# Input products that start before the normalisation, and PSUM banks in two sets of four

## The chip, the cores and the metric

One core of a Trainium2 chip runs the whole program in one launch. The metric is device time in microseconds (us), the median of several executions; lower is better.

## The reference, cut to what matters

Two stacked networks of two layers each work on 1024 tokens of 1024 channels, all in fp32. The change touches the first layer and, through the PSUM banks, every stage.

```
h    = x * rsqrt(mean(x*x, -1) + 1e-6) * norm_w        # RMS norm, per token
proj = h @ w_in                                        # q, k, v, z, q_h, f_h, i_h, g_h, gates
q, k = partial_rope(q), partial_rope(k)                # tables cos, sin from positions
a    = sliding_window_attention(q, k, v, sinks) * silu(z)
b    = hgrn2_recurrence(silu(q_h), f_h, i_h) -> norm -> * silu(g_h)
x    = x + (sigmoid(ga)*(a @ w_up_attn) + sigmoid(gh)*(b @ w_up_hgrn)) @ w_out
```

This layer runs twice. Then follow a gated MLP layer with a spatial mix in groups of 128 tokens, and a chunked attention layer in which each block of queries sees up to 640 keys with a relative bias. Since `norm_w` belongs to channels and the root to tokens, `h @ w` equals `((x * norm_w) @ w)` with each token's row multiplied by its own factor afterwards.

## The kernel before, in words

**Numbers.** A product of two fp32 tensors is made of three matmuls in the format fp32r: each operand is split into a high part (a cast) and a low part (operand minus high part), and high x high, high x low and low x high are accumulated in PSUM.

**Layout.** x and h lie channel-major: 8 tiles (index k) of 128 channels by tokens, in two halves of 512 tokens. A *unit* is one weight block with its products. `unit` (L252) and `unit_wide` (L279) work on 512 columns; `unit_tok` (L265) is token-major: h is the stationary operand, the output has 128 tokens by 256 columns, and one tile takes 24 matmuls (8 k times 3). `load_w` (L243) fetches a weight block by the SP queue into one of three `raw` buffers (`fetch_w`, L214), then `split_w` (L223) makes the parts `wh` and `wl`, of which there are 8 each.

**Order.** `run_units` (L297) writes the program unit by unit; the weights of a unit are requested two units ahead. Small work (rotary embedding, attention, recurrence, later norms) sits in *fibers*, Python generators. `tick` (L321) counts the matmuls that were written, and after each 24 of them `step` (L332) lets every fiber advance to its next `yield`. `finish` (L353) runs fibers to their end. The compiler then orders each engine's instructions by program order and readiness in its own model; TensorE's order stays nearly that of the program. `after` (L413) chains instructions behind given ones of the same engine. Copies and subtractions without a named engine go to the engine with the least booked load.

**PSUM.** Eight banks of 128 x 512 fp32 values. `mm` (L144) takes one for a unit's product, `aux` (L147) for everything else; both draw on one tag with eight buffers. `heap` (L135) gives one of 61 SBUF tiles of 128 x 512.

**The start.** `load_first` (L1139) works on the first half of the tokens in two quarters of 256, from `xq`, whose tiles hold two k each. SP fetches four x tiles, the first weight block (keys and values) in two transfers, then the second quarter's four x tiles. `squares(0)` (L1152) squares on ScalarE, adds on VectorE and sums over channels on TensorE by a matrix of ones (L1163); `rstd_of` (L386) makes the root on ScalarE and its reciprocal with one correction step on VectorE. Chained behind the root, the first weights are split on ScalarE and GpSimd; `scale(0)` (L1166) multiplies x by gain and factor and splits the result; `squares(1)` and its root follow.

**The first units.** In `layer_a` (L836) the first unit's `run` (L933) makes keys and values (`kvwork`) and the first query group (`qwork[0]`) for token tiles 0 and 1, then calls `second` (L1192), which normalises the second quarter and writes the rotary tables and constants, chained behind what ScalarE and VectorE have then, and goes on with token tiles 2 and 3. Then come the second query group (token-major), V of the recurrence (`wide_unit` with L289 to L291), and `head(0)`, whose products are L261 to L263. `swa_kv` (L545) copies keys and values out of PSUM; its fiber rotates the keys (`rope`, L529), splits them into `khl` and transposes them on TensorE (L573). The tables come from `rope_angles` (L421: a position transfer on ScalarE's queue, some forty small VectorE steps), `rope_tables` (L459) and `first_constants` (L481, three mask transfers on ScalarE's queue). `swa_q` (L593) scales queries by 1/8 as it copies them out.

**Chunked attention.** `attn2` (L1329) makes blocks of 128 queries for two heads: scores into two or four banks (L1424), VectorE's bias and maximum out of them, ScalarE's exponential, transposes (L1460), and the product with V (L1470) into one bank, which ScalarE copies out (L1476).

Of the kernel before, what the change touches and what calls it, by code (L numbers as in the profile page):

```python
# [96 lines left out]
class Net:  # L97
# [167 lines left out]
    def unit_tok(self, ps, lhs, w, t, n):  # L265
# [4 lines left out]
        for k in range(KD):  # L270
# [6 lines left out]
            nc.tensor.matmul(ps, ll[:, o : o + P], wh[:, c : c + n], start=False, stop=(k == KD - 1))  # L277

# [265 lines left out]

    def swa_kv(self, st, t, pskv):  # L545
# [6 lines left out]
        nc.scalar.copy(out=X, in_=pskv[:, 0:128])  # L552
        nc.scalar.copy(out=st["v"][:, o : o + P], in_=pskv[:, 128:256])
# [39 lines left out]
    def swa_q(self, st, l, kv, t, psq):  # L593
# [3 lines left out]
        self.nc.scalar.activation(out=X, in_=psq[:, 0:256], func=AF.Copy, scale=0.125)  # L597
# [238 lines left out]
    def layer_a(self, l, half, h, carry, merged, ready, early=None, first=None):  # L836
# [3 lines left out]
              "kvf": [], "wait": FWAIT if first else 0, "qf": [], "hf": []}  # L840
# [4 lines left out]
        def tok_unit(ap, work):  # L845
            def run(w):
                for t in range(4):
                    ps = self.mm()
                    self.unit_tok(ps[:, 0:256], h, w, 4 * half + t, 256)
                    work(4 * half + t, ps)  # L850
                    self.tick(12)
            self.units.append((lambda: self.load_w(ap, 2048), run))

        def wide_unit(ap, work):
            self.units.append((lambda: self.load_w(ap, 4096), lambda w: self.unit_wide(h, w, half, work)))

        def vwork(t, ps):
            st["V"][t] = self.heap()
            nc.scalar.copy(out=st["V"][t], in_=ps)
# [67 lines left out]
        else:  # L927

            def load():
                with self.after(first[1]):  # L930
                    return first[0], self.load_w(a["w_tok"][l, 1], 2048)

            def run(w):  # L933
                for q in range(2):
# [11 lines left out]
        wide_unit(a["w_wide"][l, 1], vwork)  # L946
        head(0)
# [191 lines left out]
    def load_first(self, res):  # L1139
# [3 lines left out]
        xs = [self.heaps(KD // 2) for _ in range(2)]  # L1143
        for k in range(KD // 2):
            nc.sync.dma_start(out=xs[0][k], in_=self.a["xq"][0, k])
        raws = self.fetch_w(self.a["w_tok"][0, 0], 2048)
# [568 lines left out]
```

## Time and profile before

| | |
|---|---|
| median of 3 runs | 3022.28 us (3022.23 to 3022.83) |
| the profiled execution | 3024.32 us |
| its span, first to last instruction | 3022.5 us |
| TensorE's mean granted clock | 0.990 of full speed |
| TensorE (PE) busy | 97% of the span |
| VectorE (DVE), ScalarE (ACT), GpSimd (POOL) busy | 56%, 48%, 36% |
| HBM read and written | 259.66 and 20.97 MB |

PE is TensorE's matmul, PEld its load of the stationary operand, SPq and ACTq a queue that issues transfers. All of the kernel's calls on VectorE, ScalarE and GpSimd go through one wrapper, so they stand under one line, L76, and are told apart by their tiles: `hp` a heap tile, `raw`, `wh`, `wl` weights, `mm` and `aux` PSUM banks. One fp32 matmul that isn't fp32r appears as two hardware matmuls, a transpose as one. A busy time that is longer than the distance to the next start means that the next instruction was already running into the pipeline: distances between starts give the pace.

### The profile page before, as it was taken

The numbers are of one execution on the slowest core, as the hardware profiler recorded it, in microseconds if no ns is written. First come the engines' busy times: TensorE is split into PE (matmuls) and PEld (weight loads), VectorE is DVE, ScalarE is ACT, GpSimd is POOL, SyncE is SP. The second block draws the span as 40 slices with busy tenths as digits, with TensorE's granted clock in tenths as the row PEclk, the third lists the DMA queues.
The fourth block names the chain that finished last, engine by engine and source line by source line (L and its number), as shares of the span: only waits on it lengthen the run. The fifth ranks groups of instructions, "written<-read, shape, count | busy, mean of one in ns | idle before, by whom it ended". The sixth has DMA issues, their size and how long they took to land.

```text
span 3022.5 us, 43638 instructions
## 1 busy us (share of the span) xinstructions
PE 2927.0 (97%) x16188; PEld 2432.3 (80%) x16188; DVE 1678.1 (56%) x3298; ACT 1449.5 (48%) x2927; POOL 1091.5 (36%) x1174
## 2 busy tenths in 40 slices
PE   6999999999999999999999999999999799999997
PEld 5887887888878888788888878888888688878777
DVE  6556745556556666665666533445344644454566
ACT  4665325642357434475334455334544545564552
POOL 4445333543435433444332233213332322232331
PEclk9999999999999999999999999999999899999999
DMA  3212242122522224212243222533234111111123
GB/s 113 84 63 93 89 147 82 66 70 91 182 70 71 73 84 151 99 70 70 74 151 132 101 92 97 166 103 129 95 116 159 56 38 60 38 59 44 64 98 112
DMA packets 101493, 283.47 MB, mean 94 GB/s; under 512 B 11288, under 2 KB 15512, under 8 KB 101280
## 3 DMA queue, kind: packets, MB, share of 16 engines
q1 hardware_dynamic: 100016, 279.51, 27.3%
q8 instruction: 128, 2.10, 0.3%
q10 hardware_dynamic: 1264, 1.17, 0.1%
q14 instruction: 85, 0.70, 0.1%
HBM read 259.66 MB, written 20.97 MB: 93 GB/s over the span
## 4 chain that ended last, share of the span: by engine, by line
PE 89%; DVE 4%; issue 2%; POOL 2%; DMA 1%; ACT 1%; SPq 0%; DVEq 0%; POOLq 0%; ACTq 0%
PE mm L261 20%; PE mm L262 20%; PE mm L263 20%; PE mm L289 3%; PE mm L290 3%; PE mm L291 3%; DVE hp L76 3%; PE aux L703 2%; PE aux L1470 2%; PE aux L1424 2%; PE mm L275 2%; PE aux L1460 2%; PE mm L276 1%; PE mm L277 1%; PE aux L634 1%
## 5 line engine op out<-in xcount | busy, mean ns | idle before, releaser
L261 PE MATMUL mm<-hp,wh 128*128 128x512 f32 (+1 forms) x2816 | 1118.8, 397 | 0.0
L262 PE MATMUL mm<-hp,wh 128*128 128x512 f32 (+1 forms) x2816 | 1093.2, 388 | 2.0 <-POOL hp L76 2.0
L263 PE MATMUL mm<-hp,wl 128*128 128x512 f32 (+1 forms) x2816 | 1093.7, 388 | 0.0
L76 POOL TENSOR_TENSOR wl<-raw,wh 128x512 fp32r<-128x512 f32 x369 | 491.3, 1334 | 800.7 <-ACT wh L76 690.7
L76 ACT CAST wh<-raw 128x512 fp32r<-128x512 f32 x584 | 360.4, 620 | 692.5 <-PE mm L262 467.1
L76 POOL TENSOR_TENSOR hp<-hp,hp 128x256 f32<-128x256 f32 (+3 forms) x347 | 380.5, 1102 | 680.1 <-DVE hp L76 240.3
L261 PEld LDWEIGHTS mm<-hp,wh 128*128 128x128 f32 x2816 | 530.7, 188 | 114.9 <-issue 11.2
L263 PEld LDWEIGHTS mm<-hp,wl 128*128 128x128 f32 x2816 | 530.0, 188 | 110.9 <-issue 0.2
L262 PEld LDWEIGHTS mm<-hp,wh 128*128 128x128 f32 x2816 | 531.1, 189 | 102.0 <-POOL hp L76 3.3
L76 DVE TENSOR_TENSOR wl<-raw,wh 128x512 fp32r<-128x512 f32 x447 | 358.8, 805 | 231.8 <-ACT wh L76 188.7
L76 DVE TENSOR_TENSOR hp<-hp,hp 128x512 f32<-128x512 f32 (+2 forms) x407 | 296.3, 737 | 154.9 <-ACT hp L76 109.3
L76 ACT ACT_TABLE_LOAD x244 | 313.1, 1283 | 22.9 <-PE mm L263 10.5
L76 DVE TENSOR_TENSOR hp<-mm,hp 128x512 f32<-128x512 f32 (+2 forms) x264 | 166.6, 637 | 161.1 <-ACT hp L76 79.3
L76 ACT ACTIVATE hp<-mm 128x512 f32<-128x512 f32 (+2 forms) x304 | 171.4, 574 | 170.0 <-PE mm L291 78.8
L76 DVE CAST wh<-raw 128x512 fp32r<-128x512 f32 x232 | 118.9, 513 | 186.9 <-PE mm L262 148.9
L76 ACT CAST hp<-hp 128x512 fp32r<-128x512 f32 (+1 forms) x206 | 116.0, 574 | 217.9 <-POOL hp L76 179.8
L76 POOL TENSOR_SCALAR sP<-sP,a2l 128x640 f32<-128x640 f32 (+4 forms) x128 | 89.0, 697 | 284.4 <-DVE a2l L76 176.7
L289 PE MATMUL mm<-wh,hp 128*128 128x512 f32 x480 | 188.1, 392 | 0.0
L290 PE MATMUL mm<-wl,hp 128*128 128x512 f32 x480 | 188.1, 392 | 0.0
L291 PE MATMUL mm<-wh,hp 128*128 128x512 f32 x480 | 187.8, 391 | 0.0
L76 ACT ACTIVATE sP<-sP,a2nm 128x640 f32<-128x640 f32 (+4 forms) x128 | 88.3, 691 | 101.1 <-DVE a2nm L76 101.0
L275 PE MATMUL mm<-wh,hp 128*128 128x256 f32 x448 | 133.7, 298 | 0.0
(186 smaller groups left out, 3406.0 us busy)
## 6 DMA issues: line engine op xcount, KB each, us to landing
raw<-in_w_ch_dram SPq DMA_DIRECT2D x128, 512.0 KB, 3.3
raw<-in_g_uz_dram SPq DMA_DIRECT2D x64, 512.0 KB, 3.3
hp<-xd SPq DMA_DIRECT2D x88, 256.0 KB, 4.2
raw<-in_w_up_dram SPq DMA_DIRECT2D x64, 256.0 KB, 2.7
raw<-in_w_o_dram SPq DMA_DIRECT2D x32, 512.0 KB, 3.3
raw<-in_g_v_dram SPq DMA_DIRECT2D x32, 512.0 KB, 4.0
raw<-in_g_o_dram SPq DMA_DIRECT2D x32, 512.0 KB, 3.8
raw<-in_w_wide_dram SPq DMA_DIRECT2D x28, 512.0 KB, 3.9
```

What stands on the lines that cost most here:

```text
L76: self.last = f(*args, **kw)
L261: nc.tensor.matmul(ps, wh[:, c : c + P], rh, start=(k == 0), stop=False)
L262: nc.tensor.matmul(ps, wh[:, c : c + P], rl, start=False, stop=False)
L263: nc.tensor.matmul(ps, wl[:, c : c + P], rh, start=False, stop=(k == nk - 1))
L275: nc.tensor.matmul(ps, lh[:, o : o + P], wh[:, c : c + n], start=(k == 0), stop=False)
L289: nc.tensor.matmul(ps, lh[:, s], wh, start=(k == 0), stop=False)
L290: nc.tensor.matmul(ps, lh[:, s], wl, start=False, stop=False)
L291: nc.tensor.matmul(ps, ll[:, s], wh, start=False, stop=(k == KD - 1))
L703: nc.tensor.matmul(ps[:, s], k[:, s], q[:, s], start=True, stop=True)
L1424: nc.tensor.matmul(ps[:, 0:w], lhs[r, o : o + P], rhs[r, k0 : k0 + w], start=(j == 0), stop=(j == 2))
L1460: nc.tensor.transpose(ps[:, j * P : (j + 1) * P], S[:, (i + j) * P : (i + j + 1) * P], self.ident)
L1470: nc.tensor.matmul(po[e * 64 : e * 64 + 64, 0:P], vv, pts[e][:, i * P : (i + 1) * P], start=(i == 0), stop=(i == nb - 1),)
```

## The change

All 8 banks were shared; now `mm` has four and `aux` has four. `load_first` no longer normalises. It makes `raw_h`, the split product of x and the gain, per quarter (`part`), interleaves the weight transfers with those of x, and returns closures. `columns(q)` puts the sum of squares per token into one PSUM column per token tile and makes the factor `rs`, and `rs8`, which is an eighth of it, with tokens on the partitions. `second` makes the second quarter's parts and squares, `constants` the rotary tables and constants. `normalise` is a fiber that makes the normalised `h` as before, for the units from `head(0)` on. The first unit works on pairs of token tiles (`pair_tok`). The first four groups of products (keys and values, both query groups, V) read `raw_h`, and `leave` multiplies by the token's factor as ScalarE copies out. A unit that finishes `normalise` stands ahead of `head(0)`.

```diff
     def mm(self):
-        return self.ps.tile([P, H], F32, tag="bank", bufs=8, name=self.name("mm"))
+        return self.ps.tile([P, H], F32, tag="mm", bufs=4, name=self.name("mm"))
     def aux(self):
-        return self.ps.tile([P, H], F32, tag="bank", bufs=8, name=self.name("aux"))
+        return self.ps.tile([P, H], F32, tag="aux", bufs=4, name=self.name("aux"))
...
+    def pair_tok(self, pss, lhs, w, ts, n):
...
+        for k in range(KD):
+            wh, wl = w[k // kg]
+            c = slice((k % kg) * n, (k % kg) * n + n)
+            for ps, t in zip(pss, ts):
+                s = slice((t % 4) * P, (t % 4) * P + P)
+                lh, ll = lhs[k][t // 4]
+                nc.tensor.matmul(ps, lh[:, s], wh[:, c], start=(k == 0), stop=False)
+                nc.tensor.matmul(ps, lh[:, s], wl[:, c], start=False, stop=False)
+                nc.tensor.matmul(ps, ll[:, s], wh[:, c], start=False, stop=(k == KD - 1))
...
+    def leave(self, st, t, out, ps):
+        if st["rs"] is None:
+            self.nc.scalar.copy(out=out, in_=ps)
+        else:
+            self.nc.scalar.activation(out=out, in_=ps, func=AF.Copy, scale=st["rs"][:, t % 4 : t % 4 + 1])
...
-        nc.scalar.copy(out=X, in_=pskv[:, 0:128])
-        nc.scalar.copy(out=st["v"][:, o : o + P], in_=pskv[:, 128:256])
+        self.leave(st, t, X, pskv[:, 0:128])
+        self.leave(st, t, st["v"][:, o : o + P], pskv[:, 128:256])
...
-        self.nc.scalar.activation(out=X, in_=psq[:, 0:256], func=AF.Copy, scale=0.125)
+        scale = 0.125 if st["rs"] is None else st["rs8"][:, t % 4 : t % 4 + 1]
+        self.nc.scalar.activation(out=X, in_=psq[:, 0:256], func=AF.Copy, scale=scale)
...
             def load():
-                with self.after(first[1]):
-                    return first[0], self.load_w(a["w_tok"][l, 1], 2048)
+                return first["w"], self.load_w(a["w_tok"][l, 1], 2048)
             def run(w):
                 for q in range(2):
-                    if q:
-                        first[2]()
-                    for wi, work in zip(w, (kvwork, qwork[0])):
-                        for t in (2 * q, 2 * q + 1):
-                            ps = self.mm()
-                            self.unit_tok(ps[:, 0:256], h, wi, t, 256)
+                    for i, (wi, work) in enumerate(zip(w, (kvwork, qwork[0]))):
+                        ts = (2 * q, 2 * q + 1)
+                        pss = [self.mm() for _ in ts]
+                        self.pair_tok([ps[:, 0:256] for ps in pss], ht, wi, ts, 256)
+                        if i == 0:
+                            first["columns"](q)
+                        for t, ps in zip(ts, pss):
                             work(t, ps)
                             if q:
                                 self.tick(12)
+                        if q == 0 and i == 0:
+                            first["second"]()
+                        if q == 0 and i == 1:
+                            first["constants"]()
+                norm = self.spawn(first["normalise"]())
+                st["norm"].append(norm)
...
         wide_unit(a["w_wide"][l, 1], vwork)
+        if first:
+            self.units.append((None, lambda w: self.finish(st["norm"])))
...
         for k in range(KD // 2):
             nc.sync.dma_start(out=xs[0][k], in_=self.a["xq"][0, k])
-        raws = self.fetch_w(self.a["w_tok"][0, 0], 2048)
+            if k % 2 == 0:
+                raws += self.fetch_w(ap[:, k * 512 : k * 512 + 1024], 1024)
...
+        def part(q, k):
+            gain = self.col("norm_w", k)
+            hi, lo = (t[:, q * Q : q * Q + Q] for t in raw_h[k][0])
+            nc.scalar.activation(out=hi, in_=view(q, k), func=AF.Copy, scale=gain)
+            nc.vector.scalar_tensor_tensor(
+                out=lo, in0=view(q, k), scalar=gain, in1=hi.bitcast(F32), op0=ALU.mult, op1=ALU.subtract
+            )
...
+        def columns(q):
+            ps = self.aux()
+            for t in range(2):
+                for i in range(2):
+                    s = i * Q + t * P
+                    nc.tensor.matmul(
+                        ps[:, t : t + 1], accs[q][:, s : s + P], self.ones_f[:, 0:1], start=(i == 0), stop=(i == 1)
+                    )
+            r = rs[:, 2 * q : 2 * q + 2]
...
+            nc.vector.tensor_scalar(out=v, in0=ps[:, 0:2], scalar1=EPS, scalar2=None, op0=ALU.add)
+            nc.scalar.activation(out=r, in_=v, func=AF.Sqrt)
+            nc.vector.reciprocal(r, r)
...
+            nc.vector.tensor_scalar(out=rs8[:, 2 * q : 2 * q + 2], in0=r, scalar1=0.125, scalar2=None, op0=ALU.mult)
+        w = []
+        for k in range(KD):
+            part(0, k)
+            if k % 4 == 0:
+                w += self.split_w(raws[k // 4], 0, None, False, ("scalar", "gpsimd"))
+        squares(0)
         def second():
-            scale(1, r)
+            for k in range(KD):
+                part(1, k)
+            squares(1)
+        def constants():
             with self.after((nc.scalar.last, nc.vector.last)):
                 self.rope_angles()
                 self.rope_tables()
                 self.first_constants()
-        return w, last, second
+        def normalise():
+            for q in range(2):
+                ps = self.aux()[:, :Q]
+                for i in range(2):
+                    nc.tensor.matmul(ps, self.ones_f, accs[q][:, i * Q : (i + 1) * Q], start=(i == 0), stop=(i == 1))
+                r = self.rstd_of(ps, Q)
+                yield
+                for k in range(KD):
+                    x = view(q, k)
+                    nc.vector.scalar_tensor_tensor(
+                        out=x, in0=x, scalar=self.col("norm_w", k), in1=r, op0=ALU.mult, op1=ALU.mult
+                    )
+                    if q == 0:
+                        res[k][0] = self.pair()
+                    hi, lo = (t[:, q * Q : q * Q + Q] for t in res[k][0])
+                    self.split(x, hi, lo)
+                    if k % 4 == 3:
+                        yield
```

In the middle of `columns`, where the diff is cut, five VectorE steps on 128 x 2 values make one correction step of the reciprocal root. `ht` is `raw_h` for the first half of the first layer and `h` everywhere else; the units of keys and values, of queries and of V read it.

## Rows read from the trace of the kernel before

**Rows 1.** The page: busy us (share of the span) and instructions of TensorE.

```profile
PE 2927.0 (97%) x16188; PEld 2432.3 (80%) x16188; DVE 1678.1 (56%) x3298; ACT 1449.5 (48%) x2927; POOL 1091.5 (36%) x1174
```

**Rows 2.** Windows: length, PE, PEld, DVE, ACT, POOL busy (count), PEclk, DMA share, GB/s.

```profile
0.00:28.60 28.60, 3.52 (x8) 2.35 (x9) 17.80 (x30) 13.90 (x27) 13.72 (x18) 1.00 0.51 177
28.60:59.50 30.90, 30.90 (x243) 30.81 (x241) 23.24 (x74) 13.51 (x36) 11.81 (x26) 1.00 0.29 93
59.50:68.00 8.50, 3.89 (x23) 2.91 (x22) 6.80 (x17) 4.29 (x23) 7.57 (x17) 0.74 0.21 76
```

**Rows 3.** Waits of TensorE over the span: us in total, times, longest us.

```profile
PE aux L1163 <- DVE hp L76: 25.1, 2, 17.4
...
PE aux L573 <- POOL khl L76: 7.6, 5, 3.0
```

**Rows 4.** Timeline to 33 us: start us, us, engine, line, operation, tiles, count.

```profile
6.27 0.63 ACT L76 ACTIVATE hp<-hp 128x512 f32<-128x512 f32 x1 [0.61 <-DMA hp<-in_xq_dram]
...
9.79 0.47 ACT L76 ACTIVATE hp<-aux,eps 128x256 f32<-128x256 f32 x1 [2.89 <-PE aux L1163]
10.16 2.16 ACT L76 CAST wh<-raw 128x512 fp32r<-128x512 f32 x4
...
10.86 5.29 POOL L76 TENSOR_TENSOR wl<-raw,wh 128x512 fp32r<-128x512 f32 x4 [9.54 <-ACT wh L76]
...
22.13 0.73 POOL L76 TENSOR_TENSOR hp<-hp,hp 128x256 fp32r<-128x256 f32 x1 [0.80 <-ACT hp L76]
...
27.15 2.08 PE L1163 MATMUL aux<-hp,ones_f 128*128 128x256 f32 x4 [17.40 <-DVE hp L76]
...
28.67 0.78 PE L275 MATMUL mm<-wh,hp 128*128 128x256 f32 x1
...
32.86 0.28 PE L275 MATMUL mm<-wh,hp 128*128 128x256 f32 x1
...
32.98 0.28 PE L276 MATMUL mm<-wl,hp 128*128 128x256 f32 x1
```

**Rows 5.** Windows of the first 10 us, columns as in rows 2.

```profile
0.00:5.00 5.00, 0.00 (x0) 0.00 (x0) 0.98 (x8) 2.74 (x4) 0.71 (x6) 1.00 0.65 216
5.00:10.00 5.00, 2.07 (x4) 1.17 (x4) 2.08 (x3) 1.47 (x4) 0.00 (x0) 1.00 0.98 320
```

**Rows 6.** Timeline from 39 to 68 us: positions, rotary tables, split keys, the next product.

```profile
39.17 0.35 ACTq L426 DMA_DIRECT2D pos<-in_pos_dram  x1
...
54.56 0.33 DVE L76 TENSOR_SCALAR cos<-angn 128x64 f32<-128x64 f32 x2
...
65.44 1.72 POOL L76 TENSOR_TENSOR khl<-hp,khl 128x128 fp32r<-128x128 f32 x4
...
67.75 0.54 PE L275 MATMUL mm<-wh,hp 128*128 128x256 f32 x1
```

**Rows 7.** Timelines from 86 to 103 us, engine by engine.

```profile
86.60 0.46 PE L614 MATMUL aux<-identr,hp 128*128 128x128 f32 x4
...
92.86 1.29 POOL L76 TENSOR_TENSOR wl<-raw,wh 128x512 fp32r<-128x512 f32 x1 [0.49 <-ACT wh L76]
...
93.10 1.33 DVE L76 CAST wh<-raw 128x512 fp32r<-128x512 f32 x1 [2.07 <-PE mm L291]
...
99.16 0.41 DVE L76 CAST wh<-raw 128x512 fp32r<-128x512 f32 x1
...
102.65 0.40 PE L261 MATMUL mm<-hp,wh 128*128 128x512 f32 x1
```

**Rows 8.** Timeline of one block of the chunked attention, from 2621 to 2625 us.

```profile
2621.49 1.09 PE L1470 MATMUL aux<-pT,hp 128*64 128x128 f32 x16
...
2622.52 1.15 PE L1424 MATMUL aux<-hp,hp 64*128 64x256 f32 x12
2622.63 0.27 ACT L76 COPY hp<-aux 128x128 f32<-128x128 f32 x1 [0.66 <-PE aux L1470]
...
2624.45 0.55 DVE L76 CUSTOM_DVE_ANT_0 sP<-aux,bias 128x384 f32<-128x384 f32 x1
```

More of the change, by code (lines that the diff above doesn't have):

```diff
@@ L839, in layer_a @@
               "b32": [None] * 4, "o": [None] * 4, "V": [None] * 4, "carry": carry,
-              "kvf": [], "wait": FWAIT if first else 0, "qf": [], "hf": []}
+              "kvf": [], "wait": FWAIT if first else 0, "qf": [], "hf": [], "rs": None, "rs8": None, "norm": []}
+        ht = h
+        if first:
+            ht, st["rs"], st["rs8"] = first["h"], first["rs"], first["rs8"]
         def col_unit(ap, cols, rhs, work):
@@ L854, in wide_unit @@
         def wide_unit(ap, work):
-            self.units.append((lambda: self.load_w(ap, 4096), lambda w: self.unit_wide(h, w, half, work)))
+            self.units.append((lambda: self.load_w(ap, 4096), lambda w: self.unit_wide(ht, w, half, work)))
         def vwork(t, ps):
             st["V"][t] = self.heap()
-            nc.scalar.copy(out=st["V"][t], in_=ps)
+            self.leave(st, t, st["V"][t], ps)
         heads = {}
@@ L1137, in dump, with load_first @@
         return norm
-    def load_first(self, res):
+    def load_first(self, raw_h, res):
         nc = self.nc
@@ L1150, in load_first @@
         nc.scalar.activation(out=warm, in_=self.eps, func=AF.Sqrt)
+        view = lambda q, k: xs[q][k // 2][:, (k % 2) * Q : (k % 2) * Q + Q]
+        rs, rs8 = (self.cp.tile([P, 4], F32, name=n) for n in ("rs", "rs8"))
+        for k in range(KD):
+            raw_h[k][0] = self.pair()
+        def part(q, k):
[5 more added lines that the diff above has]
+            )
+        accs = []
         def squares(q):
@@ L1160, in squares @@
                     nc.vector.tensor_add(acc, acc, sq)
-            ps = self.aux()[:, :Q]
-            for i in range(2):
-                nc.tensor.matmul(ps, self.ones_f, acc[:, i * Q : (i + 1) * Q], start=(i == 0), stop=(i == 1))
-            return ps
-        def scale(q, r):
-            o = slice(q * Q, (q + 1) * Q)
-            for k in range(KD):
-                x = xs[q][k // 2][:, (k % 2) * Q : (k % 2) * Q + Q]
-                nc.vector.scalar_tensor_tensor(
-                    out=x, in0=x, scalar=self.col("norm_w", k), in1=r, op0=ALU.mult, op1=ALU.mult
-                )
-                if q == 0:
-                    res[k][0] = self.pair()
-                hi, lo = res[k][0]
-                nc.scalar.copy(out=hi[:, o], in_=x)
-                e = nc.gpsimd if k % 2 else nc.vector
-                e.tensor_tensor(out=lo[:, o], in0=x, in1=hi[:, o].bitcast(F32), op=ALU.subtract)
@@ L1180, in load_first @@
-        r = self.rstd_of(squares(0), Q)
-        root = self.root
-        w = []
-        with self.tc.issue_after(root.ins):
-            for raw in raws:
-                w += self.split_w(raw, 0, None, False, ("scalar", "gpsimd"))
-        scale(0, r)
-        last = nc.scalar.last, nc.vector.last, nc.gpsimd.last
-        with self.after((root, nc.vector.last)):
-            ps = squares(1)
-        r = self.rstd_of(ps, Q)
-        def second():
-            scale(1, r)
+            accs.append(acc)
@@ L1197, in second @@
                 self.first_constants()
-        return w, last, second
+        def normalise():
[16 more added lines that the diff above has]
+                        yield
+        return {"w": w, "h": raw_h, "rs": rs, "rs8": rs8, "columns": columns, "second": second, "constants": constants,
+                "normalise": normalise}
     def load_x(self, half, res):
@@ L1504, in run @@
         h = new()
-        first = self.load_first(h)
+        first = self.load_first(new(), h)
         xin = lambda j, half: a["xT"][j, half]
```

15 lines of the change are left out of this document (14 added, 1 removed).

## The prediction, made before the changed kernel ran

> **What bounds the kernel now.** I read the page first, then the windows of the first 70 us, then who TensorE waited for, then the timeline. TensorE is busy for 2927.0 of 3022.5 us [rows 1], so a change can give back only part of the 95 us in which it idles, or take more. The windows say where: until 28.6 us the engine ran eight hardware matmuls and nothing else; from there to 59.5 us it never stopped; then it worked 3.89 of 8.5 us, and its granted clock averaged 0.74 of full speed [rows 2]. The list of waits gives two names: 25.1 us for the square sums that VectorE prepares for L1163, 7.6 us over the span for `khl`, the split rotary keys that L573 transposes [rows 3]. So two stalls can move: the normalisation ahead of the first product, and the keys behind the rotary tables. Behind them nearly every product follows directly on the one before, so a shift there reaches the end.
>
> **The sum's base.** The profiled execution took 3024.32 us around its span of 3022.5, 2.0 us over the median of 3022.28. I work out the change on the span and subtract it from the median. Below 6 us (0.2%) a measurement of this kernel can't be told from no change.
>
> **Start of the first product.** Removed from the path: both square sums with their TensorE sums, roots and rescaled splits; today the first L275 starts at 28.67 [rows 4]. In their place the first quarter needs x, its gain, one high and one low part, and the first weight half. The SP queue now sends x tile 0 (0.26 MB), raw weights (0.52), x tiles 1 and 2, raw weights, x tile 3: 2.1 MB. Transfers ran at 216 GB/s until 5 us and 320 until 10 [rows 5], so the first 1.05 MB, today four x tiles, was through at 4.9, and the last of them was used at 6.27 [rows 4]: 1.4 us later. By the same rates and lag x tile 0 and the first weights (0.79 MB) are usable at about 5.3, the second weights (1.84 MB) at 8.8, the last x tile at 9.6. A weight cast takes 2.16/4 = 0.54 us, GpSimd's low part 5.29/4 = 1.32 [rows 4]: the first low part is there at 7.2, the fourth at 12.0. I take 7.3 as TensorE's start (from 6 if the low part is early, to 11 if engine queues stand in another order). It starts at half clock (1.2 of 2.4 GHz): today 18 matmuls fit between 28.67 and 32.86, and the spacing is 0.12 from there [rows 4]. So the pair's 48 matmuls end at 7.3 + 4.2 + 30 x 0.12 = 15.1; the fourth weight half, wanted for matmul 37 at 13.7, is there. Today two such tiles end at 28.67 + 4.2 + 3.6 = 36.5: 21 us earlier. The new high and low parts (16 of each over both quarters) lie beside transfers that end later; without that cover they'd cost at most 16 x 0.54 = 8.6 us, at the wider cast's price.
>
> **columns.** Each call adds eight one-column hardware matmuls on TensorE. The trace has none so narrow. Nearest: L1163's 2.08/4 = 0.52 us for 256 columns at half clock [rows 4], L1470's 1.09/16 = 0.07 for 128 columns [rows 8]; between 0.5 and 4.2 us a call I take 1.4, since width shrinks and the stationary load stays. It waits for the square sums; ScalarE's evictions of the two key tiles wait for its root, and behind them in ScalarE's queue may stand casts for the next weights. TensorE has two more `mm` banks meanwhile, so it goes on with the first query pair: 15.1 + 1.4 + 48 x 0.12 = 22.3.
>
> **The keys: what is late next.** `constants` is chained behind ScalarE's eviction of that pair, so the position transfer, the three mask transfers on ScalarE's queue and VectorE's angle chain start at about 22.9, not 39.17: 16.3 us earlier. From there to the tables it took until 54.9, and until 67.2 to the last `khl`; the next token-major product started at 67.75 [rows 6]. I keep these durations: new 51.5. TensorE, left alone, would be there at 22.3 + 48 x 0.12 + 1.4 + 48 x 0.12 + 48 x 0.12 + 2 = 43. So of the 21 us, 16.3 survive; the keys still hold TensorE for 8 us, and the second `columns` hides in that. Bounds: 11 (VectorE busier, start late) to 24.5 (stall gone).
>
> **The normalised h.** The third and fourth unit take raw h too, so `normalise` has until the first `head` unit, L261 at 102.65 today [rows 7]. Its two sums go onto the path: 2 x 2.08 us at half clock [rows 4], 2 x 1.04 at full: +2.1. Its second quarter is started between V's two pairs, near 86.60 today, 16 us ahead of L261 [rows 7]. From root to last low part a quarter took 9.79 to 22.86 [rows 4]: 13.1, and with 1.0 for the sum and a table load or two 15 to 17. The first product uses the eight slices over 5.5 us, so the last may be late without harm. I take +2 (0 to 13): VectorE and GpSimd have weights to split just then.
>
> **Four and four.** Eight shared banks become two sets of four. The long waits of TensorE are for data, none for a bank [rows 3], so there is nothing to gain. Densest use is the chunked attention: L1470 fills one bank from 2621.49, ScalarE frees it by 2622.90, L1424 fills four from 2622.52 (the second two from about 2623.1), the last is freed at 2625.00 [rows 8]. Four auxiliary banks just suffice there. Where ScalarE is late with one, TensorE waits up to 0.7 us; with some ten to twenty such places 0 to 13, I take +3. Below zero only if the order changes. The eviction with a per-token factor is the same ScalarE instruction with another operand: nothing.
>
> **Sum.** -16.3 + 2.1 + 2 + 3 = -9.2: 3015 for the profiled execution, 3013 for the median.
>
> **The rivals.**
> 1. *The keys come soon enough.* VectorE has less beside the angles than today, where it split weights, and POOL's ropes may be shorter; then TensorE isn't stopped: -24.5 + 5.1 + 2 = -17.4 and 3005. For it: the angles start before TensorE has its weights hot. Against: every step of the chain is a dependent one. 0.18.
> 2. *Late h.* GpSimd and VectorE get in each other's way: the cast beside GpSimd's 1.29 us subtraction took 1.33 us, alone 0.41 [rows 7]. The second quarter has 16 VectorE steps or so; 0.9 each makes 14 us, less 3 of slack leaves 11 instead of 2, and 3022. 0.17. The Trainium skill (SBUF — State Buffer, Who interferes with whom) has the rule: VectorE with two SBUF inputs and a reading GpSimd exclude each other for a whole instruction. The trace's 1.33 against 0.41 agrees with such an exclusion. By that rule alone this rival's 3022 would be the forecast.
> 3. *Slower: auxiliary banks.* In chunked attention each of 64 blocks takes nine or so banks through four; today none waits. If every block lost 0.5 us to an eviction out of order, 32 us would go: 3022.3 - 12.2 + 32 = 3042. It decides the sign from (12.2 + 6)/64 = 0.3 us a block. Against: the second pair's 0.2 us of room in rows 8. 0.09.
> 4. *It doesn't start early.* If ScalarE's queue has the root and the evictions ahead of the next weights' casts, the second pair waits and `constants` with it: the gain at the keys falls to 10, and 3019. 0.06.
>
> **How the numbers follow.** The forecast has 0.50 and its own range 3008 to 3019. Faster: 0.45 of the forecast, 0.18 of rival 1, 0.05 of rival 2, 0.02 of rival 4: 0.70. Same: 0.05 + 0.10 + 0.04 = 0.19. Slower: 0.02 + 0.09 = 0.11. From 3003 to 3024 the range leaves out rival 3, the faster half of rival 1 and a tail of rival 2, together 0.2.
>
> **What would show it.** Right: the first token-major matmul near 7 us, the position transfer near 23, one gap at L573 of some 8 us ending near 51, the first `head` product near 91, L1424 and L1460 with hardly more waits than now. Wrong: L573 without a gap (rival 1), a gap ahead of the first `head` product or behind the norm's splits (2), waits of L1424, L1460 or L634 on evictions (3), a first token-major matmul or position transfer later than 30 us (4).

## The result and the profile after

The changed kernel took 2993.09 us, the median of four runs (2992.49 to 2993.65); the kernel before, beside it, 3022.56 (four runs, 3022.23 to 3024.99). The ratio is 0.9901 with a 95% interval of 0.9884 to 0.9918. That is 29.5 us, where 9.2 were forecast, and it lies outside the range. The profiled execution took 2993.03 us for a span of 2991.1.

The page of the changed kernel, TensorE's line, against [rows 1]:

```profile
PE 2927.6 (98%) x16204; PEld 2431.8 (81%) x16204; DVE 1683.4 (56%) x3322; ACT 1455.9 (49%) x2946; POOL 1098.8 (37%) x1182
```

TensorE is busy for as long as before (2927.0). What went is idle time: 3022.5 - 2927.0 = 95.5 us became 2991.1 - 2927.6 = 63.5.

To see where, I cut both traces at the same work: at the first matmul of the first, 19th, 210th, 217th, 301st, 310th, 390th and 394th product tile (an `mm` tile; numbered from 0 below). The windows of the kernel before between these cuts, columns as in [rows 2]:

```profile
0.00:28.67 28.67, 3.59 (x9) 2.42 (x9) 17.80 (x30) 13.90 (x27) 13.79 (x18) 1.00 0.51 177
28.67:116.53 87.86, 82.82 (x522) 74.03 (x521) 51.97 (x142) 43.06 (x126) 35.47 (x56) 0.96 0.25 82
116.53:1199.28 1082.75, 1071.44 (x5737) 890.37 (x5735) 666.50 (x1137) 523.72 (x1043) 460.13 (x502) 1.00 0.28 95
1199.28:1248.36 49.08, 39.47 (x202) 33.89 (x201) 34.35 (x52) 22.90 (x65) 21.45 (x39) 0.90 0.32 112
...
1733.05:1792.73 59.68, 58.15 (x277) 46.87 (x276) 20.90 (x33) 29.42 (x41) 17.81 (x16) 1.00 0.29 98
...
2341.43:2375.54 34.11, 17.74 (x109) 15.53 (x108) 21.61 (x33) 17.78 (x40) 15.74 (x13) 0.75 0.09 32
2375.54:3010.53 634.99, 622.80 (x4389) 515.35 (x4388) 327.53 (x1016) 319.43 (x792) 179.37 (x215) 0.99 0.19 64
```

The same windows of the changed kernel:

```profile
0.00:11.00 11.00, 0.00 (x1) 0.01 (x1) 1.00 (x9) 4.23 (x8) 4.10 (x9) 1.00 0.84 294
11.00:112.37 101.37, 90.77 (x545) 79.73 (x545) 71.71 (x187) 64.01 (x166) 47.80 (x73) 0.95 0.25 84
112.37:1191.63 1079.26, 1071.44 (x5737) 889.09 (x5736) 668.28 (x1138) 520.54 (x1042) 461.82 (x503) 1.00 0.29 95
1191.63:1228.53 36.90, 34.22 (x195) 29.32 (x193) 30.31 (x39) 20.04 (x60) 22.36 (x38) 1.00 0.34 113
...
1711.49:1766.54 55.05, 55.05 (x260) 45.02 (x258) 20.88 (x33) 27.44 (x37) 16.36 (x15) 1.00 0.29 101
...
2317.75:2346.21 28.46, 17.83 (x109) 16.24 (x108) 21.48 (x33) 17.49 (x40) 15.73 (x13) 0.76 0.11 38
2346.21:2978.76 632.55, 624.03 (x4388) 517.07 (x4386) 324.82 (x1015) 319.06 (x792) 179.51 (x215) 0.99 0.19 65
```

The start, the part that the change was written for, brings 116.53 - 112.37 = 4.2 us. The rest comes from places where not a line of the program differs but for the banks: 3.5 us up to tile 209, 12.2 where the second layer's second half begins (49.08 to 36.90), 4.6 in the gated MLP (59.68 to 55.05), 5.7 ahead of the chunked attention (34.11 to 28.46), 2.4 in the last stretch. Of the two stretches between that are left out of the tables, one gives 1.7 and one takes 2.5. In the second layer's 49.08 us both columns tell: idle time fell from 9.6 to 2.7 us, and the granted clock rose from 0.90 to 1.00 (1.2 GHz parts went).

What stands at two of these places shows the pattern. The timeline of TensorE before, at the second layer and ahead of the chunked attention:

```profile
1205.79 0.50 PE L383 MATMUL aux<-hp,ones_d 128*128 128x512 f32 x1 [3.48 <-DVE hp L76]
...
1227.98 0.28 PE L573 MATMUL aux<-identr,khl 128*128 128x128 f32 x1 [2.20 <-ACT khl L76]
1231.29 0.91 PE L573 MATMUL aux<-identr,khl 128*128 128x128 f32 x4 [3.03 <-POOL khl L76]
...
2346.64 0.39 PE L263 MATMUL mm<-hp,wl 128*128 128x512 f32 x1
2363.40 0.58 PE L1424 MATMUL aux<-hp,hp 64*128 64x256 f32 x2 [16.37 <-ACT hp L76]
```

And after (L383, L573 and L1424 are now L397, L594 and L1500):

```profile
1199.01 0.47 PE L397 MATMUL aux<-hp,ones_d 128*128 128x512 f32 x1 [1.82 <-DVE hp L76]
...
2322.97 0.39 PE L263 MATMUL mm<-hp,wl 128*128 128x512 f32 x1
2323.19 0.28 PE L275 MATMUL mm<-wh,hp 128*128 128x256 f32 x1
...
2328.82 0.28 PE L277 MATMUL mm<-wh,hp 128*128 128x256 f32 x1
2339.73 0.58 PE L275 MATMUL mm<-wh,hp 128*128 128x256 f32 x1 [10.63 <-DVE hp L76]
2340.25 1.69 PE L1500 MATMUL aux<-hp,hp 64*128 64x256 f32 x12
```

VectorE after, at that place:

```profile
2338.99 0.69 DVE L76 SCALAR_TENSOR_TENSOR hp<-mm,hp 128x512 fp32r<-128x512 f32 x1 [1.47 <-ACT hp L76]
```

Before, the scores L1424 came next in TensorE's order, waited for ScalarE's evictions, and 16.37 us went by. After, 48 matmuls of the next unit (L275 to L277, from 2323.19) stand ahead of the scores and run while those evictions are made; 10.63 us of waiting are left. From the last head product to the scores it is 16.8 us before (2346.64 to 2363.40) and 17.3 after (2322.97 to 2340.25); what differs is the filling. The wait that is left is that of a product, and it is for a bank: VectorE reads a head product out of its bank until 2339.68, and the next product starts right behind it. The order of TensorE is another one. Counting auxiliary tiles that stand ahead of a product tile in the kernel's own text and behind it in TensorE's order, there are 15 before and 68 after.

Now the start itself. The timeline of the changed kernel, engine by engine:

```profile
6.79 1.14 ACT L76 CAST wh<-raw 128x512 fp32r<-128x512 f32 x2 [4.12 <-DMA raw<-in_w_tok_dram]
...
9.39 1.14 ACT L76 CAST wh<-raw 128x512 fp32r<-128x512 f32 x2 [1.47 <-DMA raw<-in_w_tok_dram]
10.44 5.69 ACT L76 ACTIVATE hp<-hp,vec 128x256 fp32r<-128x256 f32 x14
...
11.00 0.58 PE L289 MATMUL mm<-wh,hp 128*128 128x256 f32 x1 [11.00 <-ACT hp L76]
...
20.08 0.39 PE L291 MATMUL mm<-wh,hp 128*128 128x256 f32 x1 [1.02 <-DVE hp L76]
...
24.80 1.05 PE L1221 MATMUL aux<-ones_f,hp 128*128 128x1 f32 x8
...
31.58 0.34 ACTq L440 DMA_DIRECT2D pos<-in_pos_dram  x1
...
43.95 0.39 PE L275 MATMUL mm<-wh,hp 128*128 128x256 f32 x1 [2.96 <-ACT hp L76]
...
55.59 0.37 PE L594 MATMUL aux<-identr,khl 128*128 128x128 f32 x1 [0.74 <-POOL khl L76]
...
59.43 0.41 PE L275 MATMUL mm<-wh,hp 128*128 128x256 f32 x1
...
80.12 0.65 PE L684 MATMUL aux<-ident,hp 128*128 128x128 f32 x4 [1.62 <-POOL hp L76]
...
97.29 0.66 PE L684 MATMUL aux<-ident,hp 128*128 128x128 f32 x4 [1.73 <-POOL hp L76]
```

The first product starts at 11.00, not 28.67: its high part waits on ScalarE behind all four weight casts, and so behind the second weight transfer (9.39). VectorE's low parts hold up the first pair of tiles once more at 20.08, and the second pair starts at 21.66. The position transfer goes out at 31.58 (39.17 before, [rows 6]), the products go on behind the keys at 59.43 (67.75 before). Then the second normalisation runs beside V and the first softmax, and L684 waits twice.

### The profile page after: what moved, and what is told of

Same layout as the page of the kernel before. It is cut to its first block, busy times and chain, and to the rows that moved or that the text cites. A ratio compares the mean times of both kernels' runs of the same rounds, so it can differ in the third digit from the quotient of the medians.

```text
span 2991.1 us, 43769 instructions
## 1 busy us (share of the span) xinstructions
PE 2927.6 (98%) x16204; PEld 2431.8 (81%) x16204; DVE 1683.4 (56%) x3322; ACT 1455.9 (49%) x2946; POOL 1098.8 (37%) x1182
## 4 chain that ended last, share of the span: by engine, by line
PE 92%; DVE 3%; issue 2%; POOL 1%; ACT 1%; DMA 1%; DVEq 0%; SPq 0%; POOLq 0%; ACTq 0%
PE mm L261 21%; PE mm L262 21%; PE mm L263 21%; PE mm L305 3%; PE mm L304 3%; PE mm L303 3%; DVE hp L76 2%; PE aux L725 2%; PE aux L1500 2%; PE aux L1546 2%; PE aux L1536 2%; PE mm L275 1%; PE mm L277 1%; PE mm L276 1%; PE aux L656 1%
## 5 line engine op out<-in xcount | busy, mean ns | idle before, releaser
L76 POOL TENSOR_TENSOR hp<-hp,hp 128x256 f32<-128x256 f32 (+3 forms) x353 | 387.6, 1105 | 672.0 <-DVE hp L76 236.3
L261 PEld LDWEIGHTS mm<-hp,wh 128*128 128x128 f32 x2816 | 530.1, 188 | 115.3 <-issue 11.5
L76 DVE TENSOR_TENSOR hp<-hp,hp 128x512 f32<-128x512 f32 (+3 forms) x401 | 289.6, 731 | 149.8 <-ACT hp L76 103.0
L275 PE MATMUL mm<-wh,hp 128*128 128x256 f32 x384 | 114.6, 298 | 13.6 <-DVE hp L76 10.6
```

Of the source, the lines that this page charges most:

```text
L76: self.last = f(*args, **kw)
L261: nc.tensor.matmul(ps, wh[:, c : c + P], rh, start=(k == 0), stop=False)
L275: nc.tensor.matmul(ps, lh[:, o : o + P], wh[:, c : c + n], start=(k == 0), stop=False)
```

## The experiments

All kernels stood beside runs of the kernel before on the chip; ratios are to these. Medians from different chips can't be compared: the kernel before took 3022.56 to 3028.55 us on them. The table gives, from each trace, when product tiles start, as a difference to the kernel before in us; its last row counts the auxiliary tiles that products pass.

| tile | before | after | banks only | start only | in order | in order, shared | 2 and 6 | 3 and 5 | 5 and 3 |
|---|---|---|---|---|---|---|---|---|---|
| 0 | 28.67 | -17.7 | -11.5 | -18.2 | -17.8 | -16.9 | -11.1 | -18.4 | -17.9 |
| 12 (V) | 75.69 | -8.8 | -4.0 | -4.7 | -4.5 | -3.6 | -1.8 | -6.0 | -11.0 |
| 18 | 116.53 | -4.2 | -3.4 | +1.7 | +1.8 | +2.7 | -2.2 | -2.4 | -2.1 |
| 209 | 1199.28 | -7.7 | -7.5 | +1.4 | +4.6 | +2.6 | +7.7 | -4.3 | +0.5 |
| 216 | 1248.36 | -19.8 | -20.3 | +2.8 | +4.8 | +5.2 | -2.1 | -14.9 | -9.2 |
| 309 | 1792.73 | -26.2 | -26.1 | +1.6 | +5.8 | +5.4 | +8.7 | -19.0 | -14.2 |
| 393 | 2375.54 | -29.3 | -28.4 | +3.2 | +6.9 | +5.6 | +15.0 | -17.7 | -23.3 |
| 462 | 2837.13 | -28.3 | -27.2 | +3.7 | +8.1 | +6.1 | +15.5 | -17.7 | +5.5 |
| last product ends | 3010.53 | -31.8 | -31.6 | +1.2 | +12.1 | +9.4 | +17.3 | -21.6 | +1.3 |
| tiles passed | 15 | 68 | 68 | 15 | 0 | 0 | 52 | 56 | 122 |

### Each half of the change alone

The kernel before with the banks divided:

```diff
-        return self.ps.tile([P, H], F32, tag="bank", bufs=8, name=self.name("mm"))
+        return self.ps.tile([P, H], F32, tag="mm", bufs=4, name=self.name("mm"))
-        return self.ps.tile([P, H], F32, tag="bank", bufs=8, name=self.name("aux"))
+        return self.ps.tile([P, H], F32, tag="aux", bufs=4, name=self.name("aux"))
```

> The kernel before with the PSUM banks divided four and four, nothing else. Theory A (with sets of their own, products of later units are placed ahead of auxiliary matmuls that wait for data): most of the 29 us, 2996 to 3001. Theory B (the early start carries the gain, the rest follows from it): no gain, 3020 to 3026. Theory C (product tiles used to wait at run time for banks that auxiliary work held): 2996 to 3001 too, and the traces' waits for evictions fall.

Measured: 2993.57 us, ratio 0.9894 (0.9882 to 0.9907).

The changed kernel with the eight shared banks of before (the same lines the other way round):

> The changed kernel with all eight banks shared again. Theory A: only the start is left, some 4 to 8 us under the kernel before, 3014 to 3019. Theory B: nearly the whole gain stays, 2993 to 2998. Theory C: as A. If the two parts add up, this gain and that of the banks alone sum to 29 us.

Measured: 3026.47 us, ratio 1.0004 (0.9995 to 1.0012).

So the banks bring all of it and the start nothing, not even the 4 to 8 us that theory A left it; theory B is out. The two columns of the table add one thing: at the first product the halves don't add up. The banks alone have the first product 11.5 us earlier, with the old normalisation in place, since products of the first pair now pass the second square sum, for which TensorE waits; the start alone has it 18.2 us earlier. At V the halves do add up (4.0 and 4.7 us against 8.8). By tile 18 they are back at -3.4 and +1.7.

### The order or the banks

The changed kernel with every instruction of TensorE chained behind the one before it in the kernel's own order; and the same with shared banks:

```diff
+    def chain(self, made):
+        if self.last is not None:
+            self.tc.add_manual_dep(
+                made.ins, self.last.ins.name,
...
+    def matmul(self, *args, **kw):
+        return self.chain(self.eng.matmul(*args, **kw))
...
+        nc.tensor = InOrder(tc.nc.tensor, tc)
```

> The changed kernel, banks four and four, with TensorE's instructions chained in the order in which the program writes them, so that no product can pass an auxiliary matmul. Theory A: the banks' gain goes, 3012 to 3020. Theory B and theory C: 2990 to 2997, since the banks and the start are as in the changed kernel.

Measured: 3037.31 us, ratio 1.0039 (1.0026 to 1.0053).

> The changed kernel with all eight banks shared and TensorE chained in the program's order: differs from the run with divided banks in that order by the banks alone. Theory A (the banks work through the order alone): the same time as that run, 3034 to 3041. Theory C (banks free at run time help by themselves): slower than that run by 5 us or more, over 3042.

Measured: 3035.55 us, ratio 1.0024 (1.0015 to 1.0034).

With the order fixed, four and four is no faster than eight shared; the gain of 1% is gone. What the division does, it does through the order, and theory C, banks that are free at run time, is out. Theory A's 3012 to 3020 was too low, since the text's order costs something by itself: with shared banks the ratio is 1.0024 in it and 1.0004 in the compiler's (the start alone). The opposite test, shared banks in the order that four and four gets, was not tried. How the order changes can be read off the built programs. In the kernel before, in the changed kernel, in both halves and in every division, tiles of one set never overtake one another: their first matmuls stand in the order in which the text asks for the tiles. With one set this holds for products and auxiliary tiles together, so that a product is in line behind auxiliary tiles that were asked for earlier; the 15 tiles that are passed in the kernel before have their own first matmul ahead of the product. With a set of its own a product isn't in that line, and the compiled order puts it ahead of auxiliary matmuls whose data are late: 61 of the 68 tiles of the changed kernel start behind a product that was asked for later. Why the compiler keeps to one line within a set was not examined.

### Other divisions

> The kernel before with two banks for products and six for auxiliary work. Theory A: two tiles are enough to place a product ahead, but only one unit ahead: a good part of the gain of four and four, 2998 to 3008. If the gain of four and four came from auxiliary work being held back by too few banks, six give none of it: 3018 to 3026. Were two banks too few for products, TensorE would wait for evictions and the time would be over 3026.

This is the kernel before with `mm` at 2 and `aux` at 6. Measured: 3041.83 us, ratio 1.0052 (1.0039 to 1.0064). Products pass 52 auxiliary tiles, and yet it is slower than before: two banks are too few for them, as the last sentence of the expectation has it; theory A's 2998 to 3008 was wrong. A line of its waits of TensorE that the kernel before doesn't have:

```profile
PE mm L261 <- DVE hp L76: 20.9, 13, 3.7
```

The longest of the 13 in the timelines of VectorE and TensorE:

```profile
1190.70 0.68 DVE L76 TENSOR_TENSOR hp<-mm,hp 128x512 f32<-128x512 f32 x1
...
1191.53 0.47 PE L261 MATMUL mm<-hp,wh 128*128 128x512 f32 x1 [3.66 <-DVE hp L76]
```

VectorE reads a product tile out of its bank until 1191.38, and the next product starts right behind it: this is a wait for a bank.

> The kernel after with three banks for products and five for the rest. Theory 'order of TensorE, with enough banks on either side': in the built order 56 auxiliary tiles are passed by later products (68 with four and four, 15 in the kernel before), so most of the four-and-four gain stays, but three product banks hold up products now and then, and five auxiliary banks let the two score tiles of a pair of heads stay adjacent. Expected 0.990 to 0.998 of the kernel before, slower than four and four by 3 to 20 us, with new waits of product lines for VectorE or ScalarE, and L1500 pairs at the pace of after (unlike five and three). Rival 'any split that keeps products out of the auxiliary queue gives the same': 0.989 to 0.991. Rival 'the split is worth something by itself only at four': above 0.999.

This is the changed kernel with 3 and 5. Measured: 3003.11 us, ratio 0.9919 (0.9904 to 0.9933), in between, as the order with enough banks on either side wants it. What one product bank is worth shows in the gap ahead of the chunked attention. With two, three, four and five of them, 0, 24, 48 and 72 products (one tile has 24) run ahead of the wait of L275 for VectorE there, and 16.8, 13.6, 10.6 and 6.8 us of it are left.

> The changed kernel with five banks for products and three for auxiliary work. Theory A: a fifth bank lets products pass more auxiliary matmuls (122 auxiliary tiles are passed in this program, 68 in the changed kernel), 2985 to 2993, unless three auxiliary banks are too few; then TensorE's or the attention's waits grow and it is over 2996.

This is the changed kernel with 5 and 3. Measured: 3024.58 us, ratio 0.9988 (0.9978 to 0.9998). It passes most tiles (122), is 23.3 us ahead at tile 393, and is 5.5 us behind at tile 462: it loses its lead in the chunked attention, where TensorE has no gap to show: 399.47 of 400 us are busy from 2400 to 2800. The busy time itself grew. Groups of TensorE by line and shape in 380 us of the chunked attention, the scores L1500, five and three:

```profile
L1500 PE MATMUL aux<-hp,hp 64*128 64x256 f32 x190 | 25.0, 309 | 0.4 <-ACT hp L76 0.4
L1500 PE MATMUL aux<-hp,hp 64*128 64x512 f32 x96 | 19.4, 433 | 0.0
L1500 PE MATMUL aux<-hp,hp 64*128 64x384 f32 x90 | 15.7, 367 | 0.1
```

And the changed kernel with four and four:

```profile
L1500 PE MATMUL aux<-hp,hp 64*128 64x256 f32 x204 | 20.2, 303 | 0.0
L1500 PE MATMUL aux<-hp,hp 64*128 64x512 f32 x96 | 15.6, 421 | 0.0
L1500 PE MATMUL aux<-hp,hp 64*128 64x384 f32 x96 | 12.5, 360 | 0.0
```

The mean of one hardly differs (309 and 303 ns), but busy time counts an overlap within a group once, and it is 60.1 us for 376 against 48.3 for 396: the scores overlap less. The kernel issues the scores of two heads in turn, one in rows 0 to 63 of the array and one in rows 64 to 127, into two auxiliary tiles. I added up, from tile 393 to 462, the time from the start of the matmul before to the start of each:

```
               scores            scores that follow   scores that follow   products
               all               another tile's score their own tile's
5 and 3        504, 75.1 us      330, 118 ns          103, 181 ns          1655, 307.6 us
4 and 4        492, 50.6 us      435,  89 ns            3, 118 ns          1656, 303.4 us
```

Of the 27.7 us by which this stretch is longer than in the changed kernel, 24.5 are the scores. With three auxiliary banks the second head's tile often has no bank when the first one's turn comes, the two are no longer issued side by side, and each then takes twice the time. The kernels with four, five and six auxiliary banks have at most 6 such places. The Trainium skill (TensorEngine Tiling (Array Packing), Key Properties) says that different tiles of the array can execute matmuls in parallel. The trace agrees, with 89 against 181 ns, and shows the condition: the two have to stand side by side in the order. That a missing bank is what parts them is argued from the number of banks alone; no run shows it.

### Where the start's lead goes

The second normalisation left out, later units of the first half reading x times the gain (`h` is `raw_h` there):

```diff
-                norm = self.spawn(first["normalise"]())
-                st["norm"].append(norm)
+                for k in range(KD):
+                    h[k][0] = ht[k][0]
```

> The changed kernel without the fiber that normalises a second time: the later units of the first half read input times gain without the token's factor, so the two sums by a matrix of ones, the roots, sixteen products and sixteen splits are left out. If this second pass is what eats the early start's lead between V and the first head unit (8.8 us over the kernel before at V, 4.2 behind it), the lead stays: 2987 to 2990. If the lead goes for another reason (the keys, the attention's softmax on GpSimd without the norm beside it), 2992 to 2994.

Measured: 2988.43 us, ratio 0.9868 (0.9854 to 0.9883). Against the changed kernel's trace tile 12 comes 1.3 us earlier, tile 18 6.4, the end 4.7: the second normalisation costs 5 us or so, between V and the second head. There TensorE is busy for 41.66 of 45.45 us in the changed kernel and for 40.38 of 40.38 in this one. So 3.8 us of the cost are idle time, all of it in waits of L684 for the softmax on GpSimd, and 1.3 are work. The first head product (94.39) waits for nothing: it is not the normalised h that comes late.

The rotary angles moved to the very start (`rope_angles` called first in `load_first` in place of `constants`):

> The changed kernel with the position transfer and the rotary angles issued at the start, where VectorE idles until 11 us; sines, cosines and masks stay where they are. If the keys behind the rotary tables hold the early start back, the gap at the key transposes and the 3.0 us gap ahead of the second query group go, the lead at V grows from 8.8 to 14 to 18 us, and some of it stays: 2984 to 2990. If the lead is lost behind V whatever its size: 2991 to 2994. If the angles delay the first low parts more than they give: over 2994.

Measured: 2998.60 us, ratio 0.9903 (0.9888 to 0.9918). The waits for the keys fall from 2.6 to 1.9 us, the gap ahead of the second query group from 3.0 to 1.3, and a longer wait takes their place; of the waits of TensorE:

```profile
PE mm L291 <- DVE hp L76: 11.3, 1, 11.3
```

VectorE works off the angle chain first, and the first quarter's low parts come only at 22.07. V starts 2.7 us later than in the changed kernel, the second head 3.6.

Three repairs of the start in one kernel: the second weight cast chained behind the first high parts, the position transfer on SyncE's queue at the start, and `constants` behind the second `columns`:

```diff
+                with self.after((nc.scalar.last,) if k else ()):
...
+        nc.sync.dma_start(out=self.pos, in_=self.a["pos"])
...
                             first["columns"](q)
+                            if q:
+                                first["constants"]()
```

> The kernel after with three edits of the start: the second weight cast follows the first half of the high parts on ScalarE, the position transfer is issued at the start on SyncE, and the rotary angles and tables follow the second pair's factors (rs). Theory 'the start is paid back later': the first product starts 1 to 2 us earlier (9 to 10 instead of 11.00), the 2.96 us gap before L275 near 44 goes, the keys (L594) start within 2 us of 52; but the second normalisation still takes the lead back before unit 17, so the end moves by less than 3 us: 2990 to 2996, ratio 0.989 to 0.9915. Rival 'the start's lead can be kept once the wait for rs is gone': 2983 to 2988, ratio 0.987 to 0.9885. The order that the compiler builds for TensorE changes too (78 auxiliary tiles passed against 68), which can move the end by some us either way.

> The kernel after, unchanged, on the chip of the two runs beside it, so that the start edits are compared on one chip. 2992 to 2996, ratio to the kernel before 0.989 to 0.991, as in its first measurement; also within 2 us of the banks alone (0.9894).

Measured on one chip: 2996.29 us for the repaired start, ratio 0.9898 (0.9884 to 0.9913), and 2995.75 for the changed kernel, 0.9892 (0.9875 to 0.9908). The edits did what they should: the first product starts at 7.90, the 2.96 us gap near 44 is gone, V starts 2.6 us earlier. The earlier first product has no part in that: VectorE's low parts come no sooner, and the second pair of tiles starts at 21.60, where it starts at 21.66 in the changed kernel. The 2.6 us come from the gap near 44. At tile 18 the lead is 0.3 us, which is what the two traces of the changed kernel differ by there (at the end they differ by 2.8, so smaller differences at the end tell nothing). Products that come earlier don't help, because TensorE then waits for the softmax beside the second normalisation.

Finally, the low parts of the second normalisation on VectorE and its high parts on ScalarE, in place of the helper's choice of engines:

```diff
-                    self.split(x, hi, lo)
+                    nc.scalar.copy(out=hi, in_=x)
+                    nc.vector.tensor_tensor(out=lo, in0=x, in1=hi.bitcast(F32), op=ALU.subtract)
```

> The kernel after, with the low parts of the second normalisation subtracted on VectorE (GpSimd has 16 of them, 0.81 us each, in 60 to 100 us) and its high parts cast on ScalarE. Theory 'GpSimd's queue is what the softmax products wait for': the waits of L684 for GpSimd (1.62 us at 80.12 and 1.73 at 97.29 in the kernel after) fall below 0.5 us each, the value unit's end and the first two head units come 2 to 4 us earlier, and the end with them, 2989 to 2992 where the kernel after has 2993 to 2996 (ratio 0.9875 to 0.989). Rival 'the normalisation as a whole is the load, wherever it runs': VectorE, at 10.0 us busy of 12.6 in that stretch, takes GpSimd's place, a wait of the same 3 us stands before L684 or before the first head product with VectorE as releaser, ratio 0.989 to 0.991. Second rival 'beside a VectorE with two operands from SBUF GpSimd itself runs slower': GpSimd's remaining multiply by sm_l (1.04 us) grows past 1.5 us.

Measured: 2997.03 us, ratio 0.9894 (0.9877 to 0.9910). L684's waits stay (1.01 us at 81.63, 2.58 at 100.84). The queue of GpSimd wasn't their cause; it has four instructions in the window from 66.92 to 81.29 where it had nine:

```profile
66.92:81.29 14.37, 13.70 (x72) 11.43 (x71) 14.04 (x36) 10.35 (x28) 4.08 (x4) 1.00 0.22 74
```

VectorE is busy for 14.04 of 14.37 us (12.55 in the changed kernel; 5.47 of 11.59 from V's first to its third tile without the normalisation). V starts 2.2 us later in this kernel, at 69.13; from its first to its third tile VectorE is busy for 13.39 of 13.67 us. So the normalisation is the load, wherever it runs. No kernel tried that computes the whole reference beat the changed kernel clearly.

## Why the prediction was wrong

**Four and four** is the step that failed. It said that the long waits are for data and none for a bank, "so there is nothing to gain", and took +3; alone it measured -32 us (3025.82 to 2993.57). The premise was right: in the trace before, at most seven of eight banks hold a live tile at once, and that for 0.9 us in all, and no wait of TensorE ends as a bank comes free. The conclusion wasn't: an engine that runs in order waits for data because of what stands next, and in the waits of [rows 3] and those at 1205.79, 1231.29 and 2363.40 independent products could have stood ahead. That they didn't was the shared set's doing. The text had the condition ("below zero only if the order changes") and gave it no chance and no price. No rival had it either. The forecast of a faster kernel came true by luck: the part that was to bring 12.2 us brings nothing, and the one that was to cost 3 brings all. To price it I'd have had to ask, for every gap of TensorE before, which products were ready, and whether they sat behind the gap only by the order.

**Start of the first product**: 7.3 forecast, with 11 as the upper end if engine queues stand in another order. They did, 11.00. With the order mended it is 7.90, so rates and lags were right (its 5.3 for the first weights should be 5.1 by its own figures, which changes nothing). The pair's end, 15.1 forecast, was not: it took until 21.66, and until 21.60 with the mended start. 26 products, not 18, run at 0.21 us or more each before the spacing is 0.12, and low parts, which the text had beside the transfers, come late from VectorE (20.08).

**columns**: 1.4 us forecast, 1.05 measured. Right.

**The keys**: -16.3 forecast, -8.3 measured (67.75 to 59.43). From the position transfer to the next product I kept 28.6 us; it took 27.9. The term that was off is the transfer's own time, 22.9 forecast and 31.58 measured. Of these 8.7 us 6.1 come from TensorE, whose second pair ends at 28.43, not 22.3: the first pair starts 3.7 late and takes 10.7 us where 7.8 were forecast. The other 2.6 are ScalarE's queue: the root and the key evictions (at 27.37) and the second quarter's squares (28.38) stand ahead of the evictions that the transfer waits for. That is rival 4's mechanism; its size (a gain of 10 at the keys) came out for this reason only in part. A second place lost 2.96 us near 44: VectorE interleaves the second factor's chain with the angles, so that it takes from 35.18 to 43.34, where it takes from 35.25 to 37.40 in the repaired start; the evictions that need it hold all four product banks meanwhile. This wait for a bank is new, like that at 2339.73, and was not foreseen.

**The normalised h**: +2.1 and +2 forecast, 4.6 measured between V (-8.8) and tile 18 (-4.2), and 5 by leaving it out (6.4 - 1.3). The size is right, the wait is another one: no product waits for a late slice of h, as the text had it, but the softmax waits (L684, 3.8 us). Rival 2 had the place. Its mechanism, VectorE and GpSimd excluding each other, shows, but doesn't decide: VectorE's sixteen rescaling steps took 0.66 us each (0.47 with GpSimd idle, at 71.19; the rival had 0.9 more for each), and 0.58 with the low parts off GpSimd, where the time stays (0.9894). GpSimd's multiply by sm_l took 1.04 us in both.

**The sum**: by its terms the start should have brought 12.2 us; at tile 18 it shows 4.2, over the banks alone 0.8, and at the end nothing that can be measured. A lead that ends in front of another wait is worth the difference to that wait. Here it is the second normalisation that takes the lead: from V to tile 18 it goes from 8.8 to 4.2 us with divided banks, and from 4.7 to a loss of 1.7 with shared ones.

**Auxiliary banks** (rival 3): with four the chunked attention hardly waits at L1500 (0.2 us in all). With three the sign is right, 27.7 us lost there, but not as waits for evictions: as scores that lost their partner.

## What to carry to other kernels

When engines run in the compiler's order, the number of buffers is not only a limit on what is live: who shares a set of buffers decides what may be ordered ahead of what. Give the work that is always ready (weight products) a set of its own, with as many banks as its evictions need, and try the neighbouring divisions: two, three, four and five for products gave 1.005, 0.992, 0.989 and 0.999 here (two in the kernel before, the others in the changed one). Before saying that a resource has nothing to give, ask of every wait for data what stood behind it and was ready. And price an earlier start at the next wait it runs into, not at the place where it begins.

## What the runs showed of the hardware

The angle steps on VectorE in the kernel with the angles first, the timeline of VectorE:

```profile
9.81 1.15 DVE L76 TENSOR_SCALAR angn<-angn 128x64 f32<-128x64 f32 x1
10.99 1.23 DVE L76 SCALAR_TENSOR_TENSOR angr<-angn,ang 128x64 f32<-128x64 f32 x1
...
13.53 0.20 DVE L76 TENSOR_SCALAR angn<-angn 128x64 f32<-128x64 f32 x1
13.76 0.22 DVE L76 SCALAR_TENSOR_TENSOR angr<-angn,angr 128x64 f32<-128x64 f32 x1
...
16.41 1.20 DVE L76 TENSOR_SCALAR angn<-angn 128x64 f32<-128x64 f32 x1
```

And GpSimd in the same kernel:

```profile
7.00 5.13 POOL L76 TENSOR_TENSOR wl<-raw,wh 128x512 fp32r<-128x512 f32 x4 [5.69 <-ACT wh L76]
15.06 3.72 POOL L76 TENSOR_TENSOR wl<-raw,wh 128x512 fp32r<-128x512 f32 x3 [2.93 <-ACT wh L76]
```

While GpSimd subtracts, the steps of 64 columns on VectorE that are shown take 1.15 to 1.23 us, about as long as one of those subtractions (5.13/4 = 1.28); between 12.13 and 15.06, with GpSimd idle, 0.20 to 0.22. Not every step is held: one at 9.58, beside GpSimd, took 0.20. I had expected this of steps with two operands; the steps with one (`angn<-angn`) are held as long, as the cast of [rows 7] was. The Trainium skill (SBUF — State Buffer, Who interferes with whom) lets whoever issues first hold the shared ports for a whole instruction, and counts tensor_scalar among those that can take them; the trace agrees.
